# Hybrid mixer layer on one core: the last projections work on two pairs of output blocks at once

## The chip, the core and the metric

The kernel runs on one core of a Trainium2 chip. Its engines are TensorE (PE, with its weight loads shown apart as PEld), VectorE (DVE), ScalarE (ACT), GpSimd (POOL) and SyncE (SP), whose queue issues every DMA of this kernel. The metric is the device time of one execution in microseconds, the median of several runs.

## The reference, cut to what matters

```python
# x: (1, 1024, 1024) float32, one layer
h = rms_norm(x, norm_w)
q, k, v, z_a, xbc, z_s, dt_raw, gate_logits = split(h @ w_in)
y_a = diff_attention(q, k, v) * silu(z_a)              # (1024, 1024)
y_s = gated_group_rms_norm(ssd_chunked(conv(xbc), dt), z_s)   # (1024, 2048)
g_a, g_s = split(gate_logits)
merged = sigmoid(g_a) * (y_a @ w_proj_attn) + sigmoid(g_s) * (y_s @ w_proj_ssd)
return x + merged @ w_out
```

The change is in the two products `y_s @ w_proj_ssd` and `y_a @ w_proj_attn`, here called the last projections.

## The kernel before, in words

**Three terms a matmul.** Every float32 operand is split into a high part (ScalarE copy to fp32r) and a low part (the difference, on VectorE or GpSimd), and a product of two operands is three matmuls: high by high, high by low, low by high (`steps3`).

**Seven products for eight.** The last projections are three stages `c`: 0 and 1 are the two halves of `y_s` (1024 of its 2048 columns each), 2 is `y_a`. Each stage multiplies a 1024x1024 weight by 1024 tokens. A *pair* is two output blocks of 128 features (`ob` and `ob + 1`) by two halves of 512 tokens: a 2x2 block matrix. It is made from seven block products instead of eight, with sums of weight blocks (made on GpSimd in `pair_splits`) and sums of operand blocks (the DRAM tensor `t_d`). A block product is 4 contraction blocks x 3 terms = 12 matmuls of 128x128 by 512 columns. A stage has four pairs, so the three stages have 84 block products.

**Order within a pair.** `ORDER` gives operand and product number: p1, p6, p2, p7, p5, p4, p3. They go into three PSUM banks: X takes p1 and then p2 on top, Y takes p6, p7 and p4, Z takes p5 and p3. Between these, `pair_step` reads the partial sums: `pc` is a copy of p1, `u6` and `u7` are `pc` plus Y, `c22` is `u7` plus Z. `BEFORE` says what must have been read before PE may add to a bank: `pc` before p2, `u6` before p7, `u7` before p4, `c22` before p3.

**Operands.** A stage needs 28 operand tiles ("forms": 7 operands x 4 contraction blocks, 256 KB each). `fill` loads a form into a free slot, and `split_in_place` makes its two parts there. The slots are the 16 tiles of `hH` and `hL` and up to 17 big buffers, so some 33. During the stage's last pair (`ob == 6`) each form's slot is given back after its use (`give_form`), and the next stage's form is loaded into it.

**Weights.** `w_loads` loads a pair's four raw weight tiles into the four raw buffers, and `pair_splits` makes seven split weight tiles, in nine slots. Each block product uses up one of them.

**What leaves a pair.** Stages 1 and 2 load, for each of the four output blocks, a gate tile `gl` and the sum so far `ac` (256 KB each, two mid buffers), combine them with the block in PSUM (`out_block`) and store the result to `acc_d`. There are 16 mid buffers (2 KB a partition) for `pc`, `u`, `gl`, `ac` and other things.

**What sets the order.** The program is written by a planner (`Plan`): tasks are generators that wait for planned times, and the order in which the plan reaches them is the fixed order of each engine's instructions. Every engine works its list strictly in that order. After the last projections comes the output projection (`final`, tiles `po`).

Of the kernel before, what the change touches and what calls it, by code (L numbers as in the profile page):

```python
# [8 lines left out]
F32 = mybir.dt.float32  # L9
# [6 lines left out]
P = 128  # L16
# [123 lines left out]
def tile_hybrid_layer(ctx: ExitStack, tc: tile.TileContext, x, norm_w, w_in, q_norm_w, k_norm_w,  # L140
# [231 lines left out]
    for src, r0 in ((w_ps, 0), (w_ps, 1024), (w_pa, 0)):  # L372
        for ob in range(0, 8, 2):
            wlist.append(pair_w(src, r0, ob * P))
# [5 lines left out]
    def w_loads(lo, hi):  # L380
        for i in range(lo, hi):
            if isinstance(wlist[i], list):
                ks = yield from pl.get(raws, 4)
                raw = [rpool.tile([P, 4, P], F32, tag="raw", name=f"rawf{i}{q}") for q in range(4)]
                raw_of[i] = (raw, ks, [load(raw[q], wlist[i][q // 2][:, :, q % 2 * P:(q % 2 + 1) * P]) for q in (0, 1, 2, 3)])
                continue
# [27 lines left out]
    def w_splits():  # L414
        for i in range(len(wlist)):
            while i not in raw_of:
                yield pl.t + 0.2
            if isinstance(wlist[i], list):
                yield from pair_splits(*raw_of.pop(i), "G" if i < NFRONT else "V")
                continue  # L420
# [18 lines left out]
    def pair_splits(raw, ks, at, eng):  # L439
# [34 lines left out]
        raws.give(ks[3], max(t, t22))  # L474

# [999 lines left out]
    def split_in_place(form, t):  # L1475
        raw = form[0][:, 1].bitcast(F32)
        t = act(form[0][:, 0], raw, AF.Copy, t)
        yield t
        return tt(form[0][:, 1], raw, form[0][:, 0].bitcast(F32), ALU.subtract, t)
# [4 lines left out]

    def products(c):
        for ob in range(0, 8, 2):
            ids = w_next(7)
            ks = []
            for q in (trs, trs, trs):
                ks.append((yield from pl.get(q, first=True)))  # L1490
            x, y, z = trt(f"pX{c}{ob}"), mmt(f"pY{c}{ob}"), trt(f"pZ{c}{ob}")
            into = {1: x, 6: y, 2: x, 7: y, 5: z, 4: y, 3: z}
            cell = {"kc": (yield from pl.get(mids)), "x": x, "ks": ks}
            if c:
                pl.spawn(pair_loads(c, ob, cell))
            if c == 2 and ob == 6:
                pl.spawn(fill_mg())
            for n, (f, p) in enumerate(ORDER):
                while p in BEFORE and BEFORE[p] not in cell:
                    yield pl.t + 0.1  # L1500
                yield from w_need(ids[n])
                wt = wts[ids[n]]
                for i in range(4):
# [5 lines left out]
                    yield from steps3(into[p], (wt[:, 0, i, :], wt[:, 1, i, :]), (form[0][:, 0], form[0][:, 1]),  # L1509
                                      i == 0 and p in (1, 6, 5), i == 3, skip_group_check=True)  # L1510
                    if ob == 6:
                        give_form(form)
                w_done(ids[n])
                pl.spawn(pair_step(c, ob, p, into[p], cell), pe_done())

    def pair_loads(c, ob, cell):
        for d, (r, h) in ((2.0, (0, 0)), (5.5, (1, 1)), (2.7, (1, 0)), (2.7, (0, 1))):
            yield pl.t + d
            grow = ob + r + (8 if c == 1 else 0)
            km = yield from pl.get(mids, 2)  # L1520
            gt, ac = midt(name=f"gl{c}{ob}{r}{h}"), midt(name=f"ac{c}{ob}{r}{h}")
            t = load(gt, gt_d[grow * P:(grow + 1) * P, h * 512:h * 512 + 512])
            t = max(t, load(ac, acc_row(ob + r, h)))
            cell["g", r, h] = (gt, ac, km, t)
# [4 lines left out]
    def pair_step(c, ob, p, ps, cell):  # L1529
        at = pe_done()  # L1530
        kx, ky, kz = cell["ks"]
        if p == 1:
            cell["c"] = midt(name=f"pc{c}{ob}")
            cell["ct"] = act(cell["c"], ps, AF.Copy, at)
        elif p in (6, 7):
            k = yield from pl.get(mids)
            u = midt(name=f"u{c}{ob}{p}")
            at = max(at, cell["ct"])
# [14 lines left out]
        elif p == 5:  # L1553
# [11 lines left out]
            cell["c22"] = at = tt(cell["x"], u, ps, ALU.add, max(at, t, cell["done", 0, 0]))  # L1565
            mids.give(k, at)
            yield from out_block(c, ob, 1, 1, cell["x"], cell, at, (trs, kx))
# [199 lines left out]
```

## Time and profile before

| | us |
|---|---|
| median of three runs | 1645.1 |
| runs, lowest to highest | 1639.2 to 1645.35 |
| the profiled execution's own time | 1646.01 |
| its span, first to last instruction | 1644.3 |

The profile is of one execution. The span is 1.7 us shorter than that execution's time, which takes in what lies before the first and after the last instruction. "Busy" of PE counts matmuls that overlap in the pipeline; where they run back to back at 2.4 GHz a 512-column matmul starts every 0.227 us though its own row says 0.39 us.

### The profile page before, as it was taken

What the parts mean: (1) busy time and instruction counts of PE and PEld (TensorE: products, weight loads), DVE (VectorE), ACT (ScalarE), POOL (GpSimd) and SP (SyncE); (2) the same over time, 40 slices, a digit from 0 to 9 for tenths busy, and PEclk for the clock granted to TensorE, in tenths of its full rate; (3) what the DMA queues carried; (4) which work ended last, traced back from release to release, by engine and by line L of the source; (5) the groups of instructions that cost most, each with busy time, mean ns of one, the idle gap of its engine ahead of it and who ended that gap; (6) DMA issues with size and microseconds to landing.
All of it is one profiled execution on the core that took longest, in us unless ns stands there. A gap on an engine that the chain in (4) does not pass through costs nothing. (4 is left out here: it accounts for less than half of the span.)

```text
span 1644.3 us, 24350 instructions
## 1 busy us (share of the span) xinstructions
PE 1598.4 (97%) x8010; PEld 1333.0 (81%) x8010; DVE 1082.8 (66%) x2011; ACT 912.4 (55%) x2215; POOL 702.4 (43%) x847
## 2 busy tenths in 40 slices
PE   7999999999999999999999999999999999999999
PEld 5788888888788888887878888888887887777887
DVE  7836568447682676876767777776656666787831
ACT  7534457455563466786666877676665634252410
POOL 4315455235541544456475546464655323222210
PEclk9999999999999999999999999999999999999999
DMA  6213343523452361426363514242425549696941
GB/s 208 91 55 109 109 150 106 169 89 119 132 182 87 107 205 43 137 62 180 97 193 113 149 51 135 81 148 96 136 84 199 192 142 346 199 316 207 322 145 64
DMA packets 223804, 236.47 MB, mean 144 GB/s; under 512 B 15285, under 2 KB 155326, under 8 KB 223678
## 3 DMA queue, kind: packets, MB, share of 16 engines
q1 hardware_dynamic: 223678, 234.93, 44.7%
q8 instruction: 63, 1.03, 0.3%
q14 instruction: 63, 0.52, 0.1%
HBM read 164.48 MB, written 70.39 MB: 143 GB/s over the span
## 5 line engine op out<-in xcount | busy, mean ns | idle before, releaser
L199 PE MATMUL pma<-w,hH 128*128 128x512 f32 x1024 | 345.1, 404 | 5.7 <-POOL w L233 5.4
L233 POOL TENSOR_TENSOR rawf<-rawf,rawf 128x512 f32<-128x512 f32 x90 | 121.0, 1345 | 262.7 <-DVE wp L233 116.7
L199 PEld LDWEIGHTS pma<-w,hH 128*128 128x128 f32 x1024 | 188.6, 189 | 40.6 <-POOL w L233 6.5
L199 PE MATMUL pma<-w,hL 128*128 128x512 f32 x512 | 207.0, 404 | 0.0
L225 ACT ACTIVATE wp<-rawf 128x512 fp32r<-128x512 f32 x180 | 109.4, 625 | 105.1 <-POOL rawf L233 72.6
L199 PE MATMUL pmz<-w,hH 128*128 128x512 f32 x512 | 164.0, 398 | 1.0 <-ACT hH L225 0.5
L233 DVE TENSOR_TENSOR wp<-rawf,wp 128x512 fp32r<-128x512 f32 x144 | 110.8, 790 | 56.0 <-ACT wp L225 55.8
L225 ACT ACTIVATE p<-p,nm 128x256 f32<-128x256 f32 (+7 forms) x128 | 98.6, 773 | 32.1 <-DVE nm L772 31.4
L199 PEld LDWEIGHTS pmz<-w,hH 128*128 128x128 f32 x512 | 96.3, 190 | 21.2 <-ACT hH L225 0.9
L225 ACT ACTIVATE w<-raw 128x512 fp32r<-128x512 f32 (+1 forms) x122 | 74.5, 625 | 69.3 <-PE po L199 30.4
L199 PEld LDWEIGHTS pma<-w,hL 128*128 128x128 f32 x512 | 96.9, 189 | 16.3
L199 PE MATMUL fYc<-ft,wp 128*128 128x512 f32 x432 | 107.0, 394 | 0.7 <-DVE fu L233 0.7
L233 POOL TENSOR_TENSOR w<-raw,w 128x512 fp32r<-128x512 f32 (+1 forms) x38 | 52.5, 1381 | 114.0 <-ACT w L225 114.0
L199 PE MATMUL pmz<-w,hL 128*128 128x512 f32 x256 | 100.9, 394 | 0.0
L199 PEld LDWEIGHTS fYc<-ft,wp 128*128 128x128 f32 x432 | 81.5, 190 | 18.1 <-DVE fu L233 1.1
L233 POOL TENSOR_TENSOR s<-rawf,rawf 128x512 f32<-128x512 f32 x30 | 39.9, 1329 | 120.1 <-DMA rawf<-in_w_proj_ssd_dram 51.7
L233 DVE TENSOR_TENSOR w<-raw,w 128x512 fp32r<-128x512 f32 (+1 forms) x84 | 65.3, 789 | 21.9 <-ACT w L225 21.7
L225 ACT ACTIVATE ab<-ab,nac 128x128 f32<-128x128 f32 x256 | 78.4, 393 | 1.7 <-POOL ab L1175 1.5
L772 DVE CUSTOM_DVE_ANT_0 p<-sc,maskb 128x512 f32<-128x512 f32 (+3 forms) x128 | 72.1, 585 | 9.7 <-issue 5.6
L199 PEld LDWEIGHTS av<-v,at 128*128 128x128 f32 x576 | 72.8, 191 | 6.9 <-ACT at L225 3.0
L265 POOL TENSOR_TENSOR rs<-rs,mhalf 128x4 f32<-128x4 f32 (+1 forms) x71 | 75.4, 1061 | 5.9
L199 PE MATMUL av<-v,at 128*128 128x128 f32 x576 | 75.1, 275 | 1.9 <-ACT at L225 1.9
(301 smaller groups left out, 4075.3 us busy)
## 6 DMA issues: line engine op xcount, KB each, us to landing
raw<-in_w_in_dram SPq DMA_DIRECT2D x104, 256.0 KB, 3.5
rawf<-in_w_in_dram SPq DMA_DIRECT2D x72, 256.0 KB, 3.8
ab<-act_d SPq DMA_DIRECT2D x32, 512.0 KB, 4.9
cv_d<-cv SPq DMA_DIRECT2D x48, 256.0 KB, 2.2
t_d<-ts SPq DMA_DIRECT2D x24, 512.0 KB, 3.2
z_d<-zs SPq DMA_DIRECT2D x32, 256.0 KB, 2.0
xr<-cv_d SPq DMA_DIRECT2D x32, 256.0 KB, 3.1
zc<-z_d SPq DMA_DIRECT2D x32, 256.0 KB, 3.0
```

The costliest lines, as they stand in the source:

```text
L199: nc.tensor.matmul(o, lhsT=lhsT, rhs=rhs, start=start, stop=stop, **kw)
L225: nc.scalar.activation(o, i, f, **kw)
L233: (nc.vector if eng == "V" else nc.gpsimd).tensor_tensor(out=o, in0=a, in1=b, op=op)
L265: nc.gpsimd.tensor_tensor(out=dst, in0=dst, in1=mhalf[:, 0:cols], op=ALU.pow)
L772: nc.vector.tensor_tensor_reduce(out=p[:, j:e], in0=sc[i][:, 0:e - j], in1=maskb[:, S - n + j:S - n + e], scale=-1.0, scalar=nms[i - 1] if ...
```

## The change

The four pairs of a stage are worked two at a time (`ob` 0 with 2, 4 with 6), block product by block product: p1 of the first, p1 of the second, p6 of the first, p6 of the second, and so on. Each takes its three banks when it first writes them, so six of the eight PSUM banks are in use. The weights of two pairs are loaded and split together (`pairs_splits`), the second pair's four raw tiles in mid buffers, and their split tiles come in the same alternating order. The gate and sum tiles of an output block are loaded by `pair_load`, which is started just before the block product that completes the block. In `split_in_place` the low part now waits (in the planner) until VectorE's planned backlog is under 5 us. Matmuls, splits, additions and transfers are the same in number and size.

```diff
@@ -370,8 +370,8 @@
     for ob in range(FRONT, 16):
         wlist += block_w(w_in, KB, C_GATE + ob * P)
     for src, r0 in ((w_ps, 0), (w_ps, 1024), (w_pa, 0)):
-        for ob in range(0, 8, 2):
-            wlist.append(pair_w(src, r0, ob * P))
+        for ob in (0, 4):
+            wlist.append([pair_w(src, r0, ob * P), pair_w(src, r0, (ob + 2) * P)])
     for n in range(2):
         wlist += wide_w(w_o, n * 512)
     raw_of, wts, w_at, w_slot = {}, {}, {}, {}
@@ -379,6 +379,16 @@
 
     def w_loads(lo, hi):
         for i in range(lo, hi):
+            if isinstance(wlist[i], list) and isinstance(wlist[i][0], list):
+                ks, raw, at = [], [], []
+                for u in range(2):
+                    for q in range(4):
+                        ks.append((yield from pl.get(mids if u else raws)))
+                    raw += [midt([P, 4, P], name=f"rawp{i}{q}") if u else
+                            rpool.tile([P, 4, P], F32, tag="raw", name=f"rawp{i}{q}") for q in range(4)]
+                    at += [load(raw[u * 4 + q], wlist[i][u][q // 2][:, :, q % 2 * P:(q % 2 + 1) * P]) for q in range(4)]
+                raw_of[i] = (raw, ks, at)
+                continue
             if isinstance(wlist[i], list):
                 ks = yield from pl.get(raws, 4)
                 raw = [rpool.tile([P, 4, P], F32, tag="raw", name=f"rawf{i}{q}") for q in range(4)]
@@ -415,6 +425,9 @@
         for i in range(len(wlist)):
             while i not in raw_of:
                 yield pl.t + 0.2
+            if isinstance(wlist[i], list) and isinstance(wlist[i][0], list):
+                yield from pairs_splits(*raw_of.pop(i))
+                continue
             if isinstance(wlist[i], list):
                 yield from pair_splits(*raw_of.pop(i), "G" if i < NFRONT else "V")
                 continue
@@ -472,6 +485,52 @@
         t = yield from split(a12, t4, eng)
         raws.give(ks[2], t)
         raws.give(ks[3], max(t, t22))
+
+    def pairs_splits(raw, ks, at):
+
+        a11, a21, a12, a22 = [[raw[q], raw[4 + q]] for q in range(4)]
+        give = lambda q, ts: (raws.give(ks[q], ts[0]), mids.give(ks[4 + q], ts[1]))
+        kt = yield from pl.get(mids, 2)
+        s3 = [midt([P, 4, P], name="s3") for _ in range(2)]
+
...
+        t0 = [max(at[0:4]), max(at[4:8])]
+        t1, t2, t3, t4 = [], [], [], []
+        for u in range(2):
+            yield t0[u]
+            t3.append(tt(s3[u], a11[u], a21[u], ALU.subtract, t0[u], "G"))
+            t1.append(tt(a21[u], a21[u], a22[u], ALU.add, t0[u], "G"))
+        u11 = yield from split(a11, t0)
+        for u in range(2):
+            t2.append(tt(a11[u], a21[u], a11[u], ALU.subtract, max(t1[u], u11[u]), "G"))
+        s2 = yield from split(a11, t2)
+        u12 = yield from split(a12, t0)
+        for u in range(2):
+            t4.append(tt(a12[u], a12[u], a11[u], ALU.subtract, max(t2[u], u12[u]), "G"))
...
     def w_next(n):
         i = used[0]
@@ -1476,65 +1535,71 @@
         raw = form[0][:, 1].bitcast(F32)
         t = act(form[0][:, 0], raw, AF.Copy, t)
         yield t
+        yield from pl.room("V", 5.0)
         return tt(form[0][:, 1], raw, form[0][:, 0].bitcast(F32), ALU.subtract, t)
 
     def split_form(c, f, i, form, t):
         t = yield from split_in_place(form, t)
         forms[c, f, i] = (form, t)
 
+    OUTS = {2: (0, 0), 5: (1, 1), 4: (1, 0), 3: (0, 1)}
+
     def products(c):
-        for ob in range(0, 8, 2):
-            ids = w_next(7)
-            ks = []
-            for q in (trs, trs, trs):
-                ks.append((yield from pl.get(q, first=True)))
-            x, y, z = trt(f"pX{c}{ob}"), mmt(f"pY{c}{ob}"), trt(f"pZ{c}{ob}")
-            into = {1: x, 6: y, 2: x, 7: y, 5: z, 4: y, 3: z}
-            cell = {"kc": (yield from pl.get(mids)), "x": x, "ks": ks}
-            if c:
-                pl.spawn(pair_loads(c, ob, cell))
-            if c == 2 and ob == 6:
+        for obs in ((0, 2), (4, 6)):
+            ids = w_next(14)
+            cells = [{}, {}]
+            if c == 2 and obs[0] == 4:
                 pl.spawn(fill_mg())
-            for n, (f, p) in enumerate(ORDER):
+            into = {1: "x", 6: "y", 2: "x", 7: "y", 5: "z", 4: "y", 3: "z"}
+            todo = [(n, u) for n in range(7) for u in range(2)]
+            for m, (n, u) in enumerate(todo):
+                f, p = ORDER[n]
+                ob, cell = obs[u], cells[u]
+                if c and m + 1 < 14 and ORDER[todo[m + 1][0]][1] in OUTS:
+                    pl.spawn(pair_load(c, obs[todo[m + 1][1]], cells[todo[m + 1][1]], *OUTS[ORDER[todo[m + 1][0]][1]]))
+                if into[p] not in cell:
+                    k = yield from pl.get(trs, first=True)
+                    cell[into[p]] = (trt(f"p{into[p]}{c}{ob}"), k)
                 while p in BEFORE and BEFORE[p] not in cell:
                     yield pl.t + 0.1
-                yield from w_need(ids[n])
-                wt = wts[ids[n]]
+                yield from w_need(ids[m])
+                wt, ps = wts[ids[m]], cell[into[p]][0]
                 for i in range(4):
                     while (c, f, i) not in forms:
                         yield pl.t + 0.1
                     form, t = forms[c, f, i]
                     if t > pl.t:
                         yield t
-                    yield from steps3(into[p], (wt[:, 0, i, :], wt[:, 1, i, :]), (form[0][:, 0], form[0][:, 1]),
+                    yield from steps3(ps, (wt[:, 0, i, :], wt[:, 1, i, :]), (form[0][:, 0], form[0][:, 1]),
                                       i == 0 and p in (1, 6, 5), i == 3, skip_group_check=True)
-                    if ob == 6:
+                    if obs[0] == 4 and u:
                         give_form(form)
-                w_done(ids[n])
-                pl.spawn(pair_step(c, ob, p, into[p], cell), pe_done())
-
-    def pair_loads(c, ob, cell):
-        for d, (r, h) in ((2.0, (0, 0)), (5.5, (1, 1)), (2.7, (1, 0)), (2.7, (0, 1))):
-            yield pl.t + d
-            grow = ob + r + (8 if c == 1 else 0)
-            km = yield from pl.get(mids, 2)
-            gt, ac = midt(name=f"gl{c}{ob}{r}{h}"), midt(name=f"ac{c}{ob}{r}{h}")
-            t = load(gt, gt_d[grow * P:(grow + 1) * P, h * 512:h * 512 + 512])
-            t = max(t, load(ac, acc_row(ob + r, h)))
-            cell["g", r, h] = (gt, ac, km, t)
+                w_done(ids[m])
+                pl.spawn(pair_step(c, ob, p, ps, cell), pe_done())
+
+    def pair_load(c, ob, cell, r, h):
+        grow = ob + r + (8 if c == 1 else 0)
+        km = yield from pl.get(mids, 2)
+        gt, ac = midt(name=f"gl{c}{ob}{r}{h}"), midt(name=f"ac{c}{ob}{r}{h}")
+        t = load(gt, gt_d[grow * P:(grow + 1) * P, h * 512:h * 512 + 512])
+        t = max(t, load(ac, acc_row(ob + r, h)))
+        cell["g", r, h] = (gt, ac, km, t)
 
     def acc_row(ob, h):
         return acc_d[ob * 256 + h * P:ob * 256 + h * P + P]
 
     def pair_step(c, ob, p, ps, cell):
         at = pe_done()
-        kx, ky, kz = cell["ks"]
+        kx, ky, kz = [cell[q][1] if q in cell else None for q in "xyz"]
         if p == 1:
+            cell["kc"] = yield from pl.get(mids)
             cell["c"] = midt(name=f"pc{c}{ob}")
             cell["ct"] = act(cell["c"], ps, AF.Copy, at)
         elif p in (6, 7):
             k = yield from pl.get(mids)
             u = midt(name=f"u{c}{ob}{p}")
+            while "ct" not in cell:
+                yield pl.t + 0.1
             at = max(at, cell["ct"])
             yield max(at, pl.t)
             cell["u", p] = (u, k, tt(u, cell["c"], ps, ALU.add, at))
@@ -1562,9 +1627,9 @@
                 return
             while ("done", 0, 0) not in cell:
                 yield pl.t + 0.1
-            cell["c22"] = at = tt(cell["x"], u, ps, ALU.add, max(at, t, cell["done", 0, 0]))
+            cell["c22"] = at = tt(cell["x"][0], u, ps, ALU.add, max(at, t, cell["done", 0, 0]))
             mids.give(k, at)
-            yield from out_block(c, ob, 1, 1, cell["x"], cell, at, (trs, kx))
+            yield from out_block(c, ob, 1, 1, cell["x"][0], cell, at, (trs, kx))
         else:
             k0, r, h, q, kq = (None, 1, 0, trs, ky) if p == 4 else ("u", 0, 1, trs, kz)
             u, k, t = (cell["c"], cell["kc"], cell["ct"]) if p == 4 else cell["u", 6]
```

Three places of the two programs' order, as the planner wrote them. First TensorE at the start of stage 2, `px`, `py`, `pz` being the banks of a pair and the number telling pairs apart; of each block product (four rows of three matmuls) only the first row is shown. Before the change, p6, p2, p7, p5, p4 of the first pair:

```order
L199 MATMUL pY_15413<-f2t_14782,wp_15406 128x512 x3
...
L199 MATMUL pX_15412<-f2b_15244,wp_15441 128x512 x3
...
L199 MATMUL pY_15413<-f2t_15273,wp_15449 128x512 x3
...
L199 MATMUL pZ_15414<-f2t_15313,wp_15455 128x512 x3
...
L199 MATMUL pY_15413<-hH,wp_15460 128x512 x3
```

With the change, p6, p6, p2, p2, p7, p7, p5:

```order
L199 MATMUL py_15494<-f2t_14749,wp_15367 128x512 x3
...
L199 MATMUL py_15515<-f2t_14749,wp_15413 128x512 x3
...
L199 MATMUL px_15433<-f2b_15119,wp_15426 128x512 x3
...
L199 MATMUL px_15469<-f2b_15119,wp_15438 128x512 x3
...
L199 MATMUL py_15494<-f2t_15174,wp_15446 128x512 x3
...
L199 MATMUL py_15515<-f2t_15174,wp_15458 128x512 x3
...
L199 MATMUL pz_15633<-f2t_15236,wp_15465 128x512 x3
```

Between a pair's p6 and its p7 stood one block product, and now stand three; each operand (`f2t`, `f2b`) serves twice before the next is wanted.

Then VectorE just before it reads that p6 (`u206` is `u6` of stage 2, pair 0; `hH` and `hL` are low parts of forms, `wp` low parts of weights, rows with `ac` or `gl` finish output blocks of the pair before). Before the change:

```order
L241 SCALAR_TENSOR_TENSOR gl1610_15329<-gl1610_15329,pY16_15201 128x512
L233 TENSOR_TENSOR wp290_15441<-rawf1322_15295,wp290_15441 128x512
L233 TENSOR_TENSOR wp291_15449<-s3_15301,wp291_15449 128x512
L233 TENSOR_TENSOR hL_112<-hL_112 128x512
L233 TENSOR_TENSOR wp292_15455<-rawf1321_15294,wp292_15455 128x512
L233 TENSOR_TENSOR hH_111<-hH_111 128x512
L233 TENSOR_TENSOR wp293_15460<-rawf1323_15296,wp293_15460 128x512
L233 TENSOR_TENSOR hL_112<-hL_112 128x512
L233 TENSOR_TENSOR hH_111<-hH_111 128x512
L233 TENSOR_TENSOR pZ16_15202<-pZ16_15202,ac1601_15359 128x512
L241 SCALAR_TENSOR_TENSOR gl1601_15358<-gl1601_15358,pZ16_15202 128x512
L233 TENSOR_TENSOR u206_15489<-pc20_15451,pY20_15413 128x512
```

With the change:

```order
L233 TENSOR_TENSOR py14_15115<-py14_15115,ac1410_15393 128x512
L241 SCALAR_TENSOR_TENSOR gl1410_15392<-gl1410_15392,py14_15115 128x512
L233 TENSOR_TENSOR wp297_15477<-rawp1281_15247,wp297_15477 128x512
L233 TENSOR_TENSOR wp298_15491<-rawp1283_15224,wp298_15491 128x512
L233 TENSOR_TENSOR py16_15138<-py16_15138,ac1610_15449 128x512
L241 SCALAR_TENSOR_TENSOR gl1610_15448<-gl1610_15448,py16_15138 128x512
L233 TENSOR_TENSOR wp299_15512<-rawp1283_15249,wp299_15512 128x512
L233 TENSOR_TENSOR u206_15523<-pc20_15471,py20_15494 128x512
L233 TENSOR_TENSOR hL_112<-hL_112 128x512
L233 TENSOR_TENSOR wp300_15540<-rawp1282_15223,wp300_15540 128x512
L233 TENSOR_TENSOR hH_111<-hH_111 128x512
```

Four low parts of forms stood ahead of `u206` among the eleven rows before it; with the change none does, and those of stage 2 that are still missing follow it.

Last the DMA queue of SP at the same crossing from stage 1 to stage 2 (`t_d`, `ya_d`: forms; `gt_d`, `acc_d` into `ac`: tiles for an output block; `acc_d<-gl`: a finished block). Before the change:

```order
L254 DMA gl1611_15302<-gt_d_86 128x512
L254 DMA ac1611_15303<-acc_d_88 128x512
L254 DMA f2t33_15308<-t_d_91 128x512
L254 DMA f2t10_15313<-t_d_91 128x512
L254 DMA f2t11_15320<-t_d_91 128x512
L254 DMA hH_111<-t_d_91 128x512
L254 DMA gl1610_15329<-gt_d_86 128x512
L254 DMA ac1610_15330<-acc_d_88 128x512
L254 DMA hL_112<-t_d_91 128x512
L254 DMA hH_111<-t_d_91 128x512
L254 DMA acc_d_88<-gl1600_15234 128x512
```

With the change:

```order
L254 DMA f2t11_15271<-t_d_91 128x512
L254 DMA f2t12_15276<-t_d_91 128x512
L254 DMA f2t13_15282<-t_d_91 128x512
L254 DMA hH_111<-t_d_91 128x512
L254 DMA acc_d_88<-gl1600_15179 128x512
L254 DMA hL_112<-t_d_91 128x512
L254 DMA hH_111<-t_d_91 128x512
L254 DMA hL_112<-t_d_91 128x512
L254 DMA hH_111<-ya_d_84 128x512
L254 DMA gl1411_15352<-gt_d_86 128x512
L254 DMA ac1411_15353<-acc_d_88 128x512
```

The same transfers stand there; the tiles of the last output blocks of stage 1 now stand behind the forms of stage 2, not among them.

## Rows read from the trace of the kernel before

**Rows 1.** The page's first two parts: busy time of TensorE and VectorE with their share of the span, and over 40 equal slices of the span the clock granted to TensorE (in tenths of 2.4 GHz).

```profile
PE   1598.4 (97%) x8010; PEld 1333.0 (81%) x8010; DVE 1082.8 (66%) x2011; ACT 912.4 (55%) x2215; POOL 702.4 (43%) x847
...
PEclk9999999999999999999999999999999999999999
```

**Rows 2.** Busy time of each engine in four stretches: the three stages of the last projections and the output projection. Columns: stretch in us, its length, busy us (and instructions) of each engine, mean granted clock as a share of 2.4 GHz, busy share of the DMA engines, GB/s moved.

```profile
core 0: us, PE busy (x) PEld busy (x) DVE busy (x) ACT busy (x) POOL busy (x), PEclk, DMA share, GB/s
1303.21:1384.27 81.06, 78.65 (x338) 63.97 (x337) 54.90 (x78) 39.75 (x73) 23.67 (x18) 0.98 0.71 242
1384.27:1466.06 81.79, 78.73 (x338) 63.93 (x337) 64.17 (x98) 27.84 (x49) 18.70 (x14) 0.98 0.76 253
1466.06:1553.86 87.80, 81.03 (x338) 65.08 (x337) 68.69 (x105) 32.52 (x59) 21.21 (x16) 0.96 0.79 272
1553.86:1641.23 87.37, 87.35 (x409) 73.14 (x407) 27.29 (x38) 10.53 (x19) 5.92 (x4) 1.00 0.39 133
```

**Rows 3.** The chain of work that ended last, three of its pieces: start, length, what. A row of x12 is one block product.

```profile
1433.58 2.72 PE pX L199 x12
1436.30 2.72 PE pY L199 x12
...
1553.86 87.36 PE po L199 x408
```

**Rows 4.** Whom TensorE waited for from 1303 to 1554 us: total, times, longest.

```profile
PE pY L199 <- DVE u L233: 3.3, 3, 2.3
PE pY L199 <- DVE wp L233: 2.4, 2, 1.9
PE pX L199 <- DVE wp L233: 2.3, 1, 2.3
PE pY L199 <- ACT wp L225: 2.2, 2, 1.8
PE pZ L199 <- DVE u L233: 2.1, 1, 2.1
```

**Rows 5.** TensorE in order of time around the crossings between stages: start, length of the merged piece, instruction, and in brackets how long TensorE was idle before it and who released it.

```profile
1379.82 1.35 PE L199 MATMUL pZ<-hH,wp 128*128 128x512 f32 x3 [2.12 <-DVE u L233]
...
1384.27 2.90 PE L199 MATMUL pX<-f1b,wp 128*128 128x512 f32 x12
...
1410.35 4.14 PE L199 MATMUL pY<-f1t,wp 128*128 128x512 f32 x10 [1.91 <-DVE wp L233]
1414.33 2.93 PE L199 MATMUL pX<-f1b,wp 128*128 128x512 f32 x12
...
1471.93 4.15 PE L199 MATMUL pY<-f2t,wp 128*128 128x512 f32 x10 [0.47 <-DVE wp L233]
1475.92 2.92 PE L199 MATMUL pX<-f2b,wp 128*128 128x512 f32 x12
1481.10 4.25 PE L199 MATMUL pY<-f2t,wp 128*128 128x512 f32 x12 [2.25 <-DVE u L233]
1485.14 1.94 PE L199 MATMUL pZ<-f2t,wp 128*128 128x512 f32 x6
1486.92 0.85 PE L199 MATMUL pZ<-hH,wp 128*128 128x512 f32 x3
```

**Rows 6.** VectorE in order of time ahead of the `u` that the wait at 1481.10 ended with (columns as in rows 5).

```profile
1473.73 0.68 DVE L233 TENSOR_TENSOR wp<-s,wp 128x512 fp32r<-128x512 f32 x1
1474.33 1.77 DVE L233 TENSOR_TENSOR hL<-hL 128x512 fp32r<-128x512 f32 x1
...
1477.83 0.68 DVE L233 TENSOR_TENSOR hL<-hL 128x512 fp32r<-128x512 f32 x1
1478.43 0.68 DVE L233 TENSOR_TENSOR hH<-hH 128x512 fp32r<-128x512 f32 x1
1479.04 0.68 DVE L233 TENSOR_TENSOR pZ<-pZ,ac 128x512 f32<-128x512 f32 x1
1479.76 0.69 DVE L241 SCALAR_TENSOR_TENSOR gl<-gl,pZ 128x512 f32<-128x512 f32 x1
1480.36 0.68 DVE L233 TENSOR_TENSOR u<-pc,pY 128x512 f32<-128x512 f32 x1
```

**Rows 7.** Stretches of 10 us (columns as in rows 2): one inside a stage and three at the crossings.

```profile
1380.00:1390.00 10.00, 10.00 (x38) 8.09 (x39) 8.79 (x16) 3.90 (x9) 0.00 (x0) 0.83 1.05 399
1430.00:1440.00 10.00, 10.00 (x46) 8.27 (x45) 7.82 (x13) 1.87 (x3) 2.58 (x2) 1.00 0.66 209
1450.00:1460.00 10.00, 10.00 (x46) 8.29 (x45) 9.93 (x17) 4.71 (x9) 1.29 (x1) 1.00 0.93 333
1470.00:1480.00 10.00, 7.65 (x24) 5.50 (x24) 9.93 (x16) 8.58 (x17) 1.61 (x1) 0.83 1.05 390
```

**Rows 8.** DMA issues from 1303 to 1554 us: transfer, how many, KB each, median us from issue to landing.

```profile
gl<-gt_d SPq DMA_DIRECT2D x32, 256.0 KB, 5.2
ac<-acc_d SPq DMA_DIRECT2D x32, 256.0 KB, 5.1
acc_d<-gl SPq DMA_DIRECT2D x28, 256.0 KB, 2.1
rawf<-in_w_proj_attn_dram SPq DMA_DIRECT2D x16, 256.0 KB, 5.4
f2t<-t_d SPq DMA_DIRECT2D x10, 256.0 KB, 5.6
```

More of the change, by code (lines that the diff above doesn't have):

```diff
@@ L474, in pair_splits, with split @@
         raws.give(ks[3], max(t, t22))
+    def pairs_splits(raw, ks, at):
[3 more added lines that the diff above has]
+        s3 = [midt([P, 4, P], name="s3") for _ in range(2)]
+        def split(src, ts):
+            done = []
+            for u in range(2):
+                k = yield from pl.get(ws)
+                n = made[0]
+                made[0] += 1
+                wt = wpool.tile([P, 2, 4, P], F32R, tag="w", name=f"wp{n}")
+                yield ts[u]
+                t = act(wt[:, 0], src[u], AF.Copy, ts[u])
+                yield t
+                t = tt(wt[:, 1], src[u], wt[:, 0], ALU.subtract, t)
+                wts[n], w_at[n], w_slot[n] = wt, t, k
+                done.append(t)
+            return done
+        t0 = [max(at[0:4]), max(at[4:8])]
[9 more added lines that the diff above has]
+        u12 = yield from split(a12, t0)
+        for u in range(2):
+            t4.append(tt(a12[u], a12[u], a11[u], ALU.subtract, max(t2[u], u12[u]), "G"))
+        give(0, [max(x) for x in zip(t4, s2)])
+        t = yield from split(s3, t3)
+        for u in range(2):
+            mids.give(kt[u], t[u])
+        t = yield from split(a21, t1)
+        give(1, [max(x) for x in zip(t, t2)])
+        t = yield from split(a22, t0)
+        give(3, [max(x) for x in zip(t, t1)])
+        t = yield from split(a12, t4)
+        give(2, t)
     def w_next(n):
```

## Prediction, made before the changed kernel ran

> **What bounds the kernel now.** I read the summary first: TensorE is busy 97% of the span and VectorE 66% [rows 1]. Nothing that another engine saves can count unless TensorE waits for it. Two things can move the time: idle or half-speed time of TensorE, and the number of its matmuls, which the change leaves as it is. The clock row has 9 in every slice [rows 1], but a slice is 41 us and hides a short drop, so I went on to stretches.
>
> The three stages of the last projections take 81.06, 81.79 and 87.80 us [rows 2]. The chain of work shows what they should take: a block product that nothing delays is 2.72 us for its 12 matmuls [rows 3]. A stage has 28, so 28 x 2.72 = 76.2 us, and the three lose 4.9, 5.6 and 11.6 us: 22.2 us of 250.65. The output projection loses nothing (87.36 us for 384 matmuls of 2.72 / 12 = 0.227 us, 87.0). So 22.2 us, 1.3% of the time, is all that a new order of these products can win. Next, where it is lost.
>
> - **Waits.** TensorE waits 3.3 + 2.4 + 2.3 + 2.2 + 2.1 = 12.3 us in five groups [rows 4]. Two are for VectorE's `u`, the sum that must be read before the next product may add to the same bank; three are for weight parts (`wp`).
> - **Half clock.** After four of these waits TensorE restarts slowly [rows 5]. Next start minus start: 12 matmuls take 1384.27 - 1379.82 = 4.45 us instead of 2.72; 10 take 1414.33 - 1410.35 = 3.98 instead of 2.27; 10 take 3.99 from 1471.93; 18 take 5.82 instead of 4.08 from 1481.10. That is 1.73, 1.71, 1.72 and 1.74, together 6.9 us. The granted clock says the same: 0.83 in two of the 10-us stretches that hold such a piece, 1.00 in those between [rows 7]. 0.83 means 3.4 us of the ten at 1.2 GHz instead of 2.4, which is 1.7 us of work lost.
> - **Rest.** 22.2 - 12.3 - 6.9 = 3.0 us: shorter gaps and restarts.
>
> All four lie where one pair or stage ends and the next begins. There VectorE has a queue. Ahead of the `u` that ended the wait before 1481.10 stand low parts of forms and two sums of the pair before, each 0.60 us after the one ahead [rows 6]; the busy time is 9.93 of 10 us from 1450 and from 1470 [rows 7]. The `u` is not slow, it is late in line. The DMA engines are full too: share 1.05 at 399 and 390 GB/s at the crossings, 0.66 at 209 within a stage [rows 7]. The cause is bunching: at a crossing a whole stage's forms, its weights and the finished blocks pass in one pair's time.
>
> **The change part by part.**
>
> *Interleaving.* From a pair's p6 to its p7 there was one block product between, and are now three (the order of TensorE above). The slack of `u6` grows from 2.72 to 8.16 us; so does that of `pc` before p2 and `c22` before p3. The wait before 1481.10 was 2.25 us beyond a slack of 2.72, so this `u` came about 5.0 us after its bank was ready. 8.16 covers that with 3.2 us over, even with the old queue. The new queue is shorter besides: no low part of a form stands ahead of `u206` among the rows shown, where four stood, worth 4 x 0.60 = 2.4 us. The two `u` groups, 3.3 + 2.1 = 5.4 us, go.
>
> *Forms and slots.* Each form serves two products in a row, so during a double pair 28 slots come free over 14 x 2.72 = 38.1 us instead of 19.0. I counted in the two programs' orders what stands in the densest run of seven block products (19.04 us): 9.7 MB of transfers before, 6.55 MB after; 37 operations of VectorE before, 30 after. At 390 GB/s 9.7 MB take 24.9 us, 5.8 too many, and 6.55 take 16.8, which fits. At 0.60 us VectorE needs 22.2 us for 37 (too much) and 18.0 for 30 (fits). So what made the weight parts late, a full queue at a crossing, should no longer be: 2.4 + 2.3 + 2.2 = 6.9 us go.
>
> *Weights of two pairs together.* The same operations in the same number, each due twice as long after its load. The second pair's four raw tiles now take mid buffers, the subject of a rival below.
>
> *The low part's wait in the plan.* It adds no instruction; it puts low parts behind more urgent work in VectorE's list. I cost it at nothing, since a form has 38 us to be made ready instead of 19. Without that cover a late low part stops TensorE as a late `wp` did, 1.1 to 2.3 us a time (2.2 us in 2 and 2.3 in 1), and 1.7 for the clock [rows 4, 5].
>
> *Gate and sum tiles.* `pair_load` is planned one block product (2.72 us) ahead of the product that completes the block; its two tiles land 5.2 and 5.1 us after issue [rows 8]. So they can arrive some 2.5 us after the product ends. Within a stage that delays only the block's own two operations, since the bank is not wanted again at once. At a crossing it can count: on SP's queue the last tiles of stage 1 now stand behind four to eight forms (see the order), and behind the sum that needs them wait VectorE's next entries, among them low parts of weights (`wp299`) and `u206`. Bounds for this: 0 if the 8.16 us of slack hold, and for c1 to c2 at most what that crossing loses now, which by rows 5 is waits of 0.47 + 2.25 and two clock episodes of 1.7, 6.2 us, and about 8 with the small gaps. The forms stand ahead in one row of eight 256-KB transfers, 2.1 MB, 5.4 us at 390 GB/s; against 8.16 + 2.72 that is nearer to the hidden end. I take 2.
>
> *Elsewhere.* The attention's tail and the start of the output projection see some instructions in another order, with the same work. I take 0, bounds -1 and +1 each. Every byte is moved in both.
>
> **The sum**, against the profiled execution's own 1646.0 us (span 1644.3): minus 22.2 (5.4 + 6.9 waits, 6.9 clock, 3.0 rest), plus 1 for gaps that stay (a third of the rest), plus 2 at c1 to c2: minus 19.2, so 1626.8. The median of the runs shown is 0.9 below that execution, so 1626. Bounds: 1624 with nothing left at the crossing, and 1622 with -1 at both ends; 1634 with the 8 and +1 at both ends.
>
> **Rivals.**
>
> A. *Half the loss stays at crossings.* The banks are no longer late but transfers are: with the DMA at 1.05 [rows 7] a load of 5.2 us [rows 8] stretches, and forms of the next stage come late. For: share 0.79 over stage 2 [rows 2], so the queue has little spare. Against: the densest seven products lose a third of their bytes. Half of 22.2 stays, 11.1: 1634 to 1637, or 1631 if it is only one crossing.
>
> B. *Gain given back.* VectorE is the limit and not the order: 37 operations in seven products become 30, but 55 in fourteen (38.1 us) were 66, and those with 1.77 us instead of 0.68 [rows 6] would make 30 into 18 + 5 x 1.1 = 23.5 us, over 19.0, by 4.5 us at each of four places: 18 us, and the result is within 8 us of 1645. Against: in rows 6 only one of the rows shown is that long.
>
> C. *Clock.* In the 10 us from 1430 and from 1450, where TensorE goes from bank to bank every 2.72 us, the clock is 1.00 [rows 3, 7]; it fell after idling [rows 5]. With six banks a small idle time at every change of bank could make it fall again and again; at 1.7 us an episode [rows 5] it takes 11 to eat 19 us, in 84 products: about 1645. The Trainium skill ("TensorE: Matmul & The Clock Gate", "A second HAM failure mode: psum-queue depth-cycling") tells of a kernel where cycling through PSUM banks made the clock oscillate. By that rule already the old kernel, which changes banks each product, should show it, and the trace does not agree within a stage.
>
> D. *Slower: mid buffers.* Of 16, the two pairs hold six (`pc` and two `u` each), and while the second pair's raw tiles and two `s3` are there, six more: four are left, two output blocks in flight. A block holds its two for 5.2 (load) + three operations of 0.7 + 2.1 (store) = 9.4 us [rows 6, 8]. Eight blocks in 38.1 us, two at a time, allow 9.5. At 11 us they take 8 / 2 x 11 = 44.0, 5.9 more per double pair, x4 (stages 1 and 2) = 23.6, plus four clock episodes 6.8: 1626 + 30 = 1656. It decides from 10.8 us. For: loads at a share of 1.05 take longer than their median. Against: the raw tiles are held for a part of the 38 us only; with three blocks in flight 14.3 us are allowed.
>
> **How the numbers follow.** The forecast (1622 to 1634) gets 0.62, A 0.14, B 0.11, C 0.04, D 0.09. A change of 0.5%, 8.2 us, is about what a measurement of this kernel can tell from none, so faster is below 1637 and slower above 1653. Faster: 0.62 and nearly all of A, less a little that A may reach beyond 1637: 0.75. Same: B, C and the rest of A, 0.16. Slower: D, 0.09. The range reaches from 1618 (below the sum's lower bound by 4, for an order elsewhere that helps more than I see) over A and the better half of B to 1641; D, C and the worse half of B, some 0.18, lie outside.
>
> **What would show it.** Right: stages of 77 to 79 us; no wait of over 1 us for `u`; at most one or two half-clock pieces from 1303 on; DMA share at the crossings below 1.0. Wrong: the forms' or `ac` loads ending TensorE's waits (A), VectorE at 9.9 of 10 us over 20 us or more with waits for `wp` or low parts (B), a clock below 1.00 with gaps under 0.5 us (C), SP idle before `gl` loads while `acc_d` stores end (D).

## The result and the profile after

The changed kernel takes 1622.98 us (median of four runs, 1620.44 to 1625.04) against 1645.22 in the same comparison: ratio 0.9869, 95% interval 0.9851 to 0.9887. The forecast was 1626, range 1618 to 1641.

The four stretches of [rows 2], in the changed kernel (same columns; the first three are the stages, the last the output projection):

```profile
1304.40:1380.56 76.16, 76.16 (x337) 63.06 (x337) 59.08 (x85) 44.69 (x81) 28.37 (x19) 1.00 0.85 288
1380.56:1456.72 76.16, 76.16 (x337) 63.06 (x337) 65.25 (x95) 32.06 (x57) 23.42 (x16) 1.00 0.82 267
1456.72:1532.88 76.16, 76.16 (x337) 63.06 (x337) 69.66 (x105) 26.22 (x46) 16.53 (x12) 1.00 0.87 287
1532.88:1620.24 87.36, 87.35 (x408) 73.11 (x407) 24.11 (x36) 10.13 (x16) 3.92 (x3) 1.00 0.39 134
```

Each stage is 76.16 us, exactly 28 products of 2.72, at a clock of 1.00: TensorE doesn't stop once in 84 block products. The groups of waits of [rows 4] have no successor (the list of TensorE's waits in these stages is empty), nor has any half-clock piece of [rows 5]. So all that could be won there is won. Read alike in both profiles, from the first matmul of the projections to the first of the output projection, they take 228.48 us instead of 250.49, which is 22.0 less; the prediction's 22.2 mixed two views of the profile, whose starts differ by 0.17 us. The first matmul starts at 1304.23 instead of 1303.21, so 1.0 us is lost ahead of it: 22.0 - 1.0 = 21.0, the difference of the spans, 1644.3 and 1623.3.

The chain of work at the start of stage 2, where one row is now a product of each pair (start, length, what):

```profile
1456.72 5.44 PE px L199 x24
1462.16 5.44 PE py L199 x24
1467.60 5.44 PE px L199 x24
1473.04 5.44 PE py L199 x24
```

They are p1, p6, p2 and p7. And VectorE there (as [rows 6]):

```profile
1468.82 0.69 DVE L241 SCALAR_TENSOR_TENSOR gl<-gl,py 128x512 f32<-128x512 f32 x1
1469.43 0.68 DVE L233 TENSOR_TENSOR wp<-rawp,wp 128x512 fp32r<-128x512 f32 x1
1470.03 0.68 DVE L233 TENSOR_TENSOR u<-pc,py 128x512 f32<-128x512 f32 x1
...
1473.04 0.68 DVE L233 TENSOR_TENSOR u<-pc,py 128x512 f32<-128x512 f32 x1
```

The first pair's p6 ends at 1462.16 + 2.72 = 1464.88 and its `u` at 1470.71: 5.8 us later. In the kernel before, p6 ended at 1471.93 + 4.15 = 1476.08 and `u` at 1481.04: 5.0 us [rows 5, 6]. So `u` is no earlier than it was; it only has 8.16 us now, with 2.3 to spare (the second pair's: 6.1 us, 2.0 to spare).

Nor have the crossings emptied. Stretches of 10 us around them, as [rows 7]:

```profile
1370.00:1380.00 10.00, 10.00 (x46) 8.29 (x45) 10.00 (x15) 9.14 (x18) 3.30 (x3) 1.00 1.05 383
1380.00:1390.00 10.00, 10.00 (x46) 8.29 (x45) 10.00 (x16) 6.98 (x14) 3.47 (x2) 1.00 0.96 319
1390.00:1400.00 10.00, 10.00 (x46) 8.29 (x45) 9.93 (x16) 2.27 (x4) 2.82 (x2) 1.00 0.54 156
...
1450.00:1460.00 10.00, 10.00 (x46) 8.29 (x45) 9.96 (x14) 9.29 (x18) 3.00 (x2) 1.00 1.05 390
1460.00:1470.00 10.00, 10.00 (x46) 8.29 (x45) 9.90 (x15) 3.50 (x7) 2.87 (x2) 1.00 0.70 239
```

VectorE is busy 9.9 of 10 us and more for 30 us, the DMA engines are at 1.05 as before, and TensorE feels neither.

### The profile page after: what moved, and what is told of

Its sections match the earlier page's. It is cut to its first block, busy times and chain, and to the rows that moved or that the text cites. A ratio compares the mean times of both kernels' runs of the same rounds, so it can differ in the third digit from the quotient of the medians.

```text
span 1623.3 us, 24344 instructions
## 1 busy us (share of the span) xinstructions
PE 1589.2 (98%) x8010; PEld 1330.2 (82%) x8010; DVE 1088.5 (67%) x2011; ACT 915.1 (56%) x2215; POOL 706.9 (44%) x847
## 4 chain that ended last, share of the span: by engine, by line
PE 73%; DVE 3%; ACT 2%; POOL 2%; DMA 2%; issue 1%; SPq 0%; POOLq 0%; DVEq 0%; ACTq 0%
PE pma L199 18%; PE py L199 6%; PE pmz L199 5%; PE po L199 5%; PE pO L199 4%; PE pz L199 4%; PE px L199 4%; PE sc L199 4%; PE av L199 4%; PE fYc L199 3%; PE fXc L199 2%; PE pg L199 2%; PE pa L208 2%; PE fZc L199 2%; PE fYg L199 1%; PE pS L199 1%
## 5 line engine op out<-in xcount | busy, mean ns | idle before, releaser
L233 POOL TENSOR_TENSOR rawf<-rawf,rawf 128x512 f32<-128x512 f32 x54 | 71.6, 1326 | 166.4 <-DVE wp L233 87.8
L225 ACT ACTIVATE wp<-rawp 128x512 fp32r<-128x512 f32 x72 | 44.2, 626 | 84.1 <-POOL rawp L233 23.9
L233 DVE TENSOR_TENSOR wp<-rawf,wp 128x512 fp32r<-128x512 f32 x72 | 59.1, 837 | 34.7 <-ACT wp L225 34.7
L225 ACT ACTIVATE wp<-rawf 128x512 fp32r<-128x512 f32 x108 | 65.9, 626 | 20.0 <-POOL rawf L233 16.4
```

The lines of the kernel that those rows point to most:

```text
L225: nc.scalar.activation(o, i, f, **kw)
L233: (nc.vector if eng == "V" else nc.gpsimd).tensor_tensor(out=o, in0=a, in1=b, op=op)
```

## The experiments

*Last projections* below is the time from the first matmul into `px` (`pX`) to the first of the output projection, in one profile: 250.5 us before the change, 228.5 after it. The other kernels, with ratios to the kernel before:

| | median us | ratio (95%) | last projections |
|---|---|---|---|
| the change | 1622.98 | 0.9869 (0.9851 to 0.9887) | 228.5 |
| e1 first half interleaved | 1631.42 | 0.9925 (0.9907 to 0.9944) | 235.8 |
| e2 second half interleaved | 1631.05 | 0.9926 (0.9907 to 0.9945) | 238.3 |
| e3 slots late | 1634.39 | 0.9945 (0.9925 to 0.9965) | 237.3 |
| e4 change without the wait in the plan | 1626.76 | 0.9899 (0.9875 to 0.9924) | 232.5 |
| e5 that wait alone | 1640.04 | 0.9978 (0.9964 to 0.9992) | 245.8 |
| e6 seven copies, before | 1662.79 | 1.0116 (1.0073 to 1.0158) | 269.8 |
| e7 seven copies, after | 1642.48 | 0.9989 (0.9973 to 1.0006) | 247.8 |
| e8 12 mid buffers | 1686.33 | 1.0263 (1.0232 to 1.0294) | 258.3 |
| e9 14 mid buffers | 1648.07 | 1.0028 (1.0014 to 1.0043) | 253.9 |
| e10 stricter wait in the plan | 1621.97 | 0.9870 (0.9855 to 0.9884) | 229.7 |
| e11 some low parts twice | 1632.26 | 0.9930 (0.9915 to 0.9945) | 236.9 |
| e12 14 mid buffers, before | 1654.91 | 1.0060 (1.0043 to 1.0077) | 255.0 |

Each edit gives the planner other times, so it moves some instructions elsewhere too; a single wait of 1 to 2 us in one of these profiles may be due to that. In e8, e9 and e12 the planner also put some of the attention's last matmuls among the first block products, so their last column holds work that the others' doesn't. No run takes out by itself the new place of the gate and sum tiles (`pair_load`) or the loading of two pairs' weights together.

**e1: only pairs 0 and 2 side by side**

```diff
-        for obs in ((0, 2), (4, 6)):
+        for obs in ((0, 2), (4,), (6,)):
```

> Only the first two pairs of each stage (ob 0 and 2) are worked side by side; ob 4 and ob 6 come one after the other as before the change, so a stage's slots are again given back within one pair, 19 us. Theory 1 (slack at the banks: three block products between p6 and p7 hide a late VectorE): of what was lost before, all but the wait at the end of stage 0 (2.1 us and 1.7 of clock) lies in the first two pairs of a stage, so 0 to 6 us above the changed kernel: 1623 to 1630. Theory 2 (bunching: what counts is that slots come free over 38 us, so that forms and weights don't crowd the crossing): half or more of the 22 us comes back, with waits for weight parts at the start of stages 1 and 2: 1632 to 1645.

TensorE's pieces that began after a wait (columns as [rows 5]):

```profile
1440.63 2.56 PE L199 MATMUL py<-f1t,wp 128*128 128x512 f32 x10 [0.87 <-DVE wp L233]
1459.17 0.50 PE L199 MATMUL px<-hL,wp 128*128 128x512 f32 x1 [1.57 <-DVE wp L233]
1464.88 0.73 PE L199 MATMUL py<-f2t,wp 128*128 128x512 f32 x2 [0.42 <-ACT wp L225]
1466.92 6.87 PE L199 MATMUL py<-f2t,wp 128*128 128x512 f32 x22 [1.31 <-DVE wp L233]
```

1631.42 lies just between the two theories. No wait for `u` is left and all are for weight parts, at the last pair of stage 1 and the start of stage 2: the kind of theory 2, a third of the loss. None of the four is over 1.6 us, so the kind rests on all four being for weight parts.

**e2: only pairs 4 and 6 side by side**

```diff
-        for obs in ((0, 2), (4, 6)):
+        for obs in ((0,), (2,), (4, 6)):
```

> Only the last two pairs of each stage (ob 4 and 6) are worked side by side; ob 0 and ob 2 come one after the other. Slots come free over 38 us as with the whole change. Theory 1 (slack at the banks): the first two pairs of stages 1 and 2 lose again what they lost before, some 15 us with the clock: 1634 to 1641. Theory 2 (bunching): the crossings stay clear and TensorE hardly waits: 1623 to 1630.

```profile
1310.69 0.97 PE L199 MATMUL py<-hH,wp 128*128 128x512 f32 x3 [0.37 <-DVE u L233]
1388.37 0.97 PE L199 MATMUL py<-hL,wp 128*128 128x512 f32 x3 [0.88 <-DVE u L233]
1468.41 5.49 PE L199 MATMUL py<-f2t,wp 128*128 128x512 f32 x12 [3.21 <-DVE u L233]
1486.23 2.57 PE L199 MATMUL py<-f2t,wp 128*128 128x512 f32 x10 [0.87 <-DVE wp L233]
```

1631.05 lies between the two theories again, as the mirror image: three waits for `u` in first pairs of a stage, the kind of theory 1, one of them with a whole product at half clock behind it (5.49 us for 12 matmuls). Neither theory alone holds: with the first pairs one by one the sums are late, with the last pairs one by one the weights are, and each costs some 8 us of the 22. Which part of working two pairs side by side kept the weights in time, e1 doesn't tell: it takes away the slack, the loading of two pairs' weights together and the long release of slots at once. e3 takes the release alone.

**e3: slots given back late**

```diff
-                    if obs[0] == 4 and u:
-                        give_form(form)
+                if obs[0] == 4 and m >= 7:
+                    for i in range(4):
+                        give_form(forms[c, ORDER[m - 7][0], i][0])
```

> The whole change, but in the last two pairs of a stage the slots of a form are given back seven block products later than they could be, one form group for each of the last seven products: within 19 us as before the change. Theory 1 (slack at the banks): TensorE hardly waits, 0 to 4 us above the changed kernel: 1622 to 1627. Theory 2 (bunching): forms or weight parts come late at both crossings, 8 us or more back: 1631 to 1645.

By this edit the first form group is given back six block products later than in the change, the last no later at all. The time is theory 2's number. VectorE and TensorE in its stage 2:

```profile
1485.46 3.44 DVE L233 TENSOR_TENSOR hH<-hH 128x512 fp32r<-128x512 f32 x2
1488.82 0.68 DVE L241 SCALAR_TENSOR_TENSOR px<-gl,px 128x512 f32<-128x512 f32 x1
1489.54 0.69 DVE L233 TENSOR_TENSOR gl<-px,ac 128x512 f32<-128x512 f32 x1
1490.15 0.68 DVE L233 TENSOR_TENSOR hL<-hL 128x512 fp32r<-128x512 f32 x1
1490.74 0.69 DVE L233 TENSOR_TENSOR wp<-rawp,wp 128x512 fp32r<-128x512 f32 x1
1491.35 1.28 DVE L233 TENSOR_TENSOR u<-pc,py 128x512 f32<-128x512 f32 x2
```

```profile
1464.52 5.72 PE L199 MATMUL py<-f2t,wp 128*128 128x512 f32 x24 [1.35 <-ACT f2t L225]
...
1492.17 1.62 PE L199 MATMUL py<-f2t,wp 128*128 128x512 f32 x3 [5.61 <-DVE u L233]
```

The `u` of a p7 that ended at 1478.24 ends at 1492.03, 13.8 us later; the 8.16 us hide the rest and TensorE waits 5.61. With the old bunching, low parts stand ahead of the `u` again, eight of the fifteen operations that began after that p7, and four of these took 1.0 to 1.7 us instead of 0.68; three products of slack are not enough. What came late is a form (1.35 us) and this sum; none of TensorE's waits here is for a weight part, so it isn't shown that the long release of slots is what kept the weights in time.

**e4 and e5: the wait in the plan.** e4 takes it out of the change, e5 puts it alone into the kernel before.

```diff
         yield t
-        yield from pl.room("V", 5.0)
```

> The whole change without the low part's wait in the plan (the line in split_in_place). The prediction costed this line at nothing: 1621 to 1626, no wait of over 1 us from 1303 us on. Rival: the line keeps low parts from standing ahead of the sums that free the banks, and without it part of the waits for u come back, 3 to 12 us: 1626 to 1635.

> The kernel before with one part of the change alone, the low part's wait in the plan. If the line is worth by itself what it is worth within the change (3.8 us in e4), 1639 to 1643, and the u at the start of stage 2 comes earlier. If pairs worked one by one leave no time to make low parts later, the low parts become late instead: 1644 to 1655, with waits for hH, hL or f.

e4's profile has one wait, and half clock after it:

```profile
1465.36 6.85 PE L199 MATMUL py<-f2t,wp 128*128 128x512 f32 x22 [2.18 <-DVE wp L233]
```

Its four runs are 1623.4, 1624.3, 1629.2 and 1629.6, so this wait may not come in every run; the profiled run is one of the long ones. It is a wait for a weight part, not for the `u` that the rival named. By the last projections the line is worth 4.0 us in that profile, and alone 0.22% (0.08 to 0.36), 3.6 us. The interval of e4 overlaps that of the change a little (0.9875 to 0.9887), so its size within the change is not settled; that it isn't worth nothing in the kernel before is shown by e5.

How it is worth something there is not as expected. The `u` at the start of stage 2 does come earlier (TensorE waits 1.34 us, not 2.25), but other waits came, and in all TensorE waits 12.4 us in e5's profile against 12.3. What is less is the half clock. One piece after a wait is slow, where four were; the second row here, after a like wait, is not:

```profile
1469.60 4.10 PE L199 MATMUL pY<-f2t,wp 128*128 128x512 f32 x10 [1.56 <-DVE wp L233]
...
1477.76 3.00 PE L199 MATMUL pY<-f2t,wp 128*128 128x512 f32 x12 [1.34 <-DVE u L233]
```

Over all runs the mean granted clock is 0.9953 in e5 (ten runs) and 0.9931 in the kernel before (eighteen), 3.6 us of work at full clock, as much as the gain. Why the clock fell less often there is open.

**e10: the limit at 2 us instead of 5.**

> The changed kernel with the low part waiting until VectorE's planned backlog is under 2 us instead of 5. If the line's worth (3.8 us, e4) grows on with a stricter limit there is nothing more to win, since TensorE waits for nothing in the last projections: 1620 to 1626. If the low parts now come late, waits for hH, hL or f: 1627 to 1640.

The ratio is that of the change. One wait of 0.95 us for a `u` stands in its profile, where the change had none, and the projections start 3.5 us earlier.

**e6 and e7: `pc` copied seven times**

```diff
-            cell["ct"] = act(cell["c"], ps, AF.Copy, at)
+            for _ in range(7):
+                cell["ct"] = at = act(cell["c"], ps, AF.Copy, at)
```

> The kernel before, with the copy pc of p1 in the last projections made seven times over (six needless ScalarE copies in each of 12 pairs; VectorE and the transfers are not touched). One copy is some 0.6 us, so pc is ready some 4.3 us after p1. Theory 1 (slack at the banks): p2 must follow after 2.72 us, so TensorE waits 1.5 to 2 us in each of 12 pairs, and the clock falls after some of them: 1660 to 1690.

> The changed kernel with the same seven copies. Theory 1: p2 follows p1 only after 8.16 us, so 4.3 us are hidden, and the second pair's seven copies, behind the first's, end some 6.2 us after its p1 and are hidden too: 1621 to 1628. If the slack doesn't carry that far, waits for pc appear: over 1632.

TensorE's waits (total, times, longest), first e6, then e7:

```profile
PE pX L199 <- ACT pc L225: 19.7, 11, 3.4
```

```profile
PE px L199 <- DVE wp L233: 4.6, 1, 4.6
PE px L199 <- ACT wp L225: 3.2, 3, 2.0
PE px L199 <- ACT pc L225: 2.9, 2, 2.1
```

ScalarE in e7, ahead of the waits of 2.02 us (ended at 1356.58) and 4.65 us (ended at 1471.88):

```profile
1351.64 4.37 ACT L225 ACTIVATE pc<-px 128x512 f32<-128x512 f32 x7
1355.90 0.62 ACT L225 ACTIVATE wp<-rawp 128x512 fp32r<-128x512 f32 x1
...
1465.30 0.63 ACT L225 ACTIVATE hH<-hH 128x512 fp32r<-128x512 f32 x1 [3.69 <-DMA hH<-ya_d]
1465.83 1.14 ACT L225 ACTIVATE wp<-rawp 128x512 fp32r<-128x512 f32 x2
```

The wait for `pc` is 1.75 us in most pairs of e6, as computed, and 2.9 us in all after the change: the slack at the banks is real and hides what it should. Yet e7 lost 19.3 us in the last projections, as much as e6, and its expectation was wrong. ScalarE is busy 142.9 us of 247.8 (103.1 of 228.5 without the copies), and its list also makes the high parts of weights and forms. The waits of 2.02 and 0.97 us for a weight's high part end with one that stood right behind seven copies. So slack in front of one reader doesn't make room in its engine's list. The longest wait, 4.65 us, is another matter: no copy ran in the 25 us before it, ScalarE had stood still for a form's load, and the weight part stood behind that form in its list and then behind six operations in VectorE's. Whether the copies brought that about is not shown.

**e8, e9 and e12: fewer mid buffers**

```diff
-NBIG, NW, NRAW, NMID, NSM = 17, 9, 4, 16, 8
+NBIG, NW, NRAW, NMID, NSM = 17, 9, 4, 14, 8
```

(12 in e8; e12 is the kernel before with 14.)

> The changed kernel with 12 mid buffers instead of 16. By the prediction's rival D (16 are just enough, 9.5 us allowed for 9.4) it loses over 20 us: 1645 or more. If the raw tiles give their buffers back early, as the forecast has it, a loss of 0 to 12 us: 1622 to 1635.

> The changed kernel with 14 mid buffers instead of 16; with 12 it took 63 us more (e8). If 16 are just enough, as rival D had it, part of that loss is here too: 1635 to 1660. If 16 leave room to spare, 1622 to 1630.

> The kernel before with 14 mid buffers instead of 16, as a control to e9 (the changed kernel with 14: 25 us more than with 16). If it is the change that needs the two buffers (a second pair's raw tiles, s3, pc and u), one pair at a time does without: 1640 to 1650. If both need them, 1655 or more.

e9, TensorE among the first products (two of its pieces of attention) and at a p4 of stage 1; then ScalarE and VectorE ahead of that p4:

```profile
1308.76 1.72 PE L199 MATMUL av<-v,at 128*128 128x128 f32 x14
...
1323.18 1.95 PE L199 MATMUL av<-v,at 128*128 128x128 f32 x16
...
1468.45 1.65 PE L199 MATMUL py<-hH,wp 128*128 128x512 f32 x3 [15.52 <-DVE u L233]
```

```profile
1452.00 0.63 ACT L225 ACTIVATE hL<-hL 128x512 fp32r<-128x512 f32 x1 [3.97 <-DMA hL<-t_d]
...
1452.67 0.69 DVE L233 TENSOR_TENSOR hL<-hL 128x512 fp32r<-128x512 f32 x1 [3.65 <-ACT hL L225]
1453.28 1.28 DVE L233 TENSOR_TENSOR wp<-rawp,wp 128x512 fp32r<-128x512 f32 x2
1456.87 0.70 DVE L233 TENSOR_TENSOR hH<-hH 128x512 fp32r<-128x512 f32 x1 [2.31 <-ACT hH L225]
...
1467.71 1.28 DVE L233 TENSOR_TENSOR u<-pc,py 128x512 f32<-128x512 f32 x2
```

VectorE stands still twice, 6.0 us in all, for low parts whose forms have not landed, and has sixteen operations between the first of these and the `u`. This one place costs the wait of 15.5 us and 2.5 us of half clock behind it. Most of the rest of the 25.5 us is 6.6 us of the attention's matmuls, which with 14 buffers are still to do when the projections begin. Together they make the changed kernel 0.3% slower than the old one with 16: rival D's direction and rough size, two buffers away. They don't show D's mechanism, since TensorE waits for no gate or sum tile here but for a `u` behind late low parts. The kernel before loses 0.6% with 14, so with 14 in both the changed kernel would still be some 0.3% ahead, by the two ratios. With 12 the last projections lose 29.8 us and another 31 us are lost before they begin (`px` starts at 1335.1), so e8 says less on this change. Why the plan puts the low parts so early with 14 was not looked into.

**e11: 21 low parts made twice**

```diff
+        if n == 2:          # n is 2 for one form in four
+            k = yield from pl.get(mids)
+            t = tt(midt(name="again"), raw, form[0][:, 0].bitcast(F32), ALU.subtract, t)
+            mids.give(k, t)
```

> The changed kernel with the low part of one in four forms made twice (the first time into a mid buffer that nobody reads): 21 more operations of VectorE, 0.6 us each, 12.6 us over the three stages, four or five of them at each crossing. If the slack in front of the sums (2 us and more left) and the low priority of low parts carry this: 1622 to 1630. If VectorE's full stretches at the crossings (9.9 of 10 us) are the limit, as rival B has it, each crossing loses what it is given and the clock falls: 1630 to 1645.

```profile
1448.91 1.38 PE L199 MATMUL py<-hL,wp 128*128 128x512 f32 x3 [3.87 <-DVE u L233]
1491.30 0.93 PE L199 MATMUL py<-hH,wp 128*128 128x512 f32 x3 [2.40 <-DVE u L233]
```

By the time the second reading holds. 12.6 us more on VectorE cost 8.5 us here. VectorE is busy 215.5 of 236.9 us, so it has time in the mean; at the crossing from stage 1 to 2, where about 2 us of slack were left, it has too little. The spare buffer it takes may count too; this run doesn't part them.

## Why the prediction was right, and where its steps were not

- **What could be won, and that it would be:** all of the loss in the last projections came back, 22.0 us read alike in both profiles. Of the sum's two reserves, 1 us for gaps and 2 at c1 to c2, neither was needed; the start of the projections lost 1.0 us, at the bound set for the attention's tail. Forecast 19.2, measured 21.0 between the profiles and 22.2 between the medians.
- **Interleaving gives the sums 8.16 us:** right. The wait at that `u` is gone, waits for `u` come back where the first pairs are taken one by one (e2), and e6 and e7 show the slack hide a late reader in ten of twelve pairs.
- **The queue ahead of `u` is 2.4 us shorter, and 8.16 us would do even with the old queue:** wrong. `u206` came 5.8 us after its product, 5.0 before the change; from the product's end on, no low part of a form stood ahead instead of three, but four weight parts and four operations on finished blocks instead of two and two. And e3, with the old release of slots, waits 5.6 us beyond the slack. I had read one place in the order, where the kernel has a dozen.
- **Forms and slots over 38 us keep the weights in time:** the waits for weight parts went, as forecast, and come back with the last pairs one by one (e1); a short release of slots alone costs as much but by a late form and a late sum (e3), so what kept the weights in time stays open. How the crossing would look was wrong. I expected the DMA share below 1.0 and VectorE no longer full; they are at 1.05 and 9.9 of 10, as before. The term that failed is VectorE's 18.0 us for 30 operations at 0.60: from 1368 to 1387 us, 26 operations take 19.0 us, 0.73 each. The work isn't thinner where it is thickest; each piece of it is wanted later.
- **The low part's wait in the plan costs nothing and, by the sum, brings nothing:** mis-sized. It is worth 3.6 us alone (e5), as far as the runs show by the clock, and about 4 in the change (e4, not settled).
- **Rivals.** A and B: their signs (full DMA, full VectorE) came without their result, since slack took them up; e11 shows B begin with 12.6 us more. C: the clock is 1.00 through three stages with six banks in turn, and in the kernel before it fell only after TensorE had waited. The Trainium skill's case ("TensorE: Matmul & The Clock Gate", "A second HAM failure mode: psum-queue depth-cycling") is one of short idle times between groups of matmuls while the banks are cycled, not of cycling alone as the prediction read it; without idle time it doesn't arise here. D: its price per block was too low, since a block takes 4.0 (load) + 2.1 + 4.7 (store, rows below) = 10.8 us, the very point at which I let it decide, and nothing was lost with 16 buffers. With 14 the loss is of D's size, but TensorE waits for a `u` there (e9).

```profile
gl<-gt_d SPq DMA_DIRECT2D x32, 256.0 KB, 3.8
ac<-acc_d SPq DMA_DIRECT2D x32, 256.0 KB, 4.0
acc_d<-gl SPq DMA_DIRECT2D x27, 256.0 KB, 4.7
```

These are the DMA issues of the changed kernel's last projections, as [rows 8].

## What to carry to other kernels

When TensorE waits for the reader of a partial sum, look at how long the sum lay ready and not only at the reader's queue: working two independent chains in turn turned 2.7 us of slack into 8.2, and the reader could stay as late as it was. Slack and an even supply are both needed (e1, e2 and e3 each gave back 7 to 10 us of the 22), and the slack is bought with buffers: try the neighbouring buffer counts, since with two fewer the gain of 22 us over the old kernel with 16 became a loss of 5. Where a list is worked in order, an instruction that waits for a load holds up all behind it (e9), so what is wanted late should be put late; here that was worth some 4 us (e4, e5), in e5 through the clock and not through shorter waits.

## What the runs showed of the hardware that was not expected

The same 256-KB transfers, issued in another order on the same queue, landed after other times: the gate and sum tiles in 3.8 and 4.0 us instead of 5.2 and 5.1, the stores in 4.7 instead of 2.1. So the time for which a block holds its buffers, summed from the medians of the old order, was off by 1.4 us (9.4 for 10.8). Why the stores slowed was not tried.
